# Hybrid S5 and gated-DeltaNet layer: 32x32 triangular blocks inverted on GpSimd, the decay matrix from a masked scan, and new operation durations in the model that places background work

## The chip, the cores and the metric

The kernel runs on one core of a Trainium2 chip. The metric is the device time of one execution in microseconds (us), as a median of several runs. The engines are TensorE (PE; its weight loads are listed apart as PEld), VectorE (DVE), ScalarE (ACT), GpSimd (POOL) and SyncE (SP), which issues most of the transfers between the chip's main memory (DRAM) and its on-chip memory.

## What is computed

The reference is one residual layer on x of 1024 rows by 2048 columns, in float32. Cut to what matters here:

```python
h = rmsnorm(x, ln_w)
proj = h @ w_in          # split: u_s, z_s (1024 each), q, k, v, z_d (1024 each), beta, a (8 each), gate_s, gate_d (2048 each)
# S5: 64 groups x 64 complex states, a linear recurrence along the rows, then GELU, GLU, SiLU gate
y_s = s5_mixer(u_s, z_s, ...) @ s5_w_up
# DeltaNet, 8 heads of 128: short convolution, SiLU, l2norm, then the chunked delta rule
decay = exp(where(causal, gc[:, None] - gc[None, :], -inf))      # gc = cumsum(g) in a chunk
a_mat = where(strict, beta[:, None] * (k @ k.T) * decay, 0)
sol = triangular_solve(I + a_mat, [v * beta, k * beta * exp(gc)])
y_d = ... @ dn_w_up
x = x + (sigmoid(gate_s) * y_s + sigmoid(gate_d) * y_d) @ w_out
out = rmsnorm(x, final_norm_w)
```

## The kernel before

**Passes and foreground.** The rows are worked in two passes of 512 (`NPASS`, `T`). In a pass the foreground is a stream of PE matmuls of 128x128 weights against 512 columns. Each weight chunk is split into a high and a low float32r part (`whi` by ACT, `wlo` by DVE, from `raw`, which SP loads), and the sum takes three matmuls per 128x128 block. `plan` lists the projection tiles in order: `ba`, then for each head the tiles k, q, v, z and two of gate_d with one S5 input tile `u` between, then the `zs` tiles, the DeltaNet up projection `ud`, the gate `gs`, the S5 GLU `glu`, the S5 up projection `us`, and the output projection. A tile of w_in takes 48 matmuls, one of `glu`, `ud` or `us` 24.

**Background and planner.** All else is written as Python generators in lanes (`lanes`): `epi`, `io`, `chain`, `prep`, `tab`, `s5`, `out`, `x`. After each three foreground matmuls `pump()` gives every lane one chance to emit its next step. `step()` decides with a clock that runs while the program is written: `Clock` and `Timed` charge each instruction a duration from `COST` and keep for each engine the modelled time, and for each piece of memory when it was last written and read. A step is emitted once the modelled PE clock has passed the time at which the step before has its result, and if DVE's clock isn't too far ahead of PE's. The result is a fixed order on each engine; the clock has no part in the run. Two rules matter below. `late(lane, h)` says that head h of `prep` or `chain` is overdue (by more than `LATE`, in heads, against `now`, the place in the plan); while one is, `step()` holds back `s5` and `tab` altogether:

```python
            elif lane in ("s5", "tab") and job[0] >= 0 and late_any():
                return
```

And `drain(lane)` emits all that a lane still holds, at once, in a row. It stands ahead of `ud` for `prep` and `chain`, and ahead of the first `glu` tile for `s5` (with the tables of `tab` interleaved), since `glu` multiplies the S5 result.

**S5** (`s5_gen`, `s5_table`). An S5 group t holds 4 pairs in 2 slots, 8 groups and 32 pairs in a pass. A slot has two pairs: PE makes the inputs of both in PSUM, then for each pair DVE rotates (two products, two sums), scans twice, rotates back (two products, two sums) and copies the carries; PE makes the slot's outputs and ACT copies them out of PSUM. In the first pass each pair also needs a table of cosines and sines (`s5_table`), made by DVE and ACT, and stored in `cs_d`. A group ends with GELU and a split into two parts, four stores to `yg_d`; after the eighth, `yg_load` loads all into the blocks `G0a` and `G0b`. The working tiles of S5 lie in `G0a` and `G0b` too.

**DeltaNet** (`d_views`, `gates_prep`, `d_prep`, `d_chain`). Four chunks of 128 rows are worked side by side. `gates_prep` makes the log decays `gt` for all heads. `d_prep(h)`, in lane `prep`, one head after another on shared tiles, makes the decay matrix E: GpSimd multiplies the high and low part of the log decays into a causal mask (`dhl`), PE sums with `after_r` (four matmuls of 256 columns), ACT takes the exponential. Then come the k by k and k by q products, `LU` (the strictly upper part of a_mat, transposed), and the inverse of the unit triangle: `LU` is stored to `lu_d`, 32 diagonal blocks of 16x16 are loaded one to a partition, GpSimd inverts them by 15 substitution steps of two operations each, the inverses and their transposes go out to `tu_d` and come back as `Tm` and `U`; PE then merges 16 to 32 (two steps of 16 and 32 matmuls of 32x32, with `off16` and `id32` between), 32 to 64 and 64 to 128. `d_chain(h)` runs the recurrence over the chunks.

In the profile nearly all instructions have the line of the helper in `Timed` that issues them (L135), so groups are told apart by their tiles: M holds DeltaNet's tiles, G0a and G0b those of S5, X and Y the foreground's inputs.

Of the kernel before, what the change touches and what calls it, by code (L numbers as in the profile page):

```python
# [36 lines left out]
P = 128  # L37
# [56 lines left out]
class Timed:  # L94
    def __init__(self, eng, key, clock):
        self.eng, self.key, self.clock = eng, key, clock

    def __getattr__(self, name):
# [4 lines left out]
        def g(*a, **k):  # L103
# [6 lines left out]
            if self.key == "PE":  # L110
                if name == "transpose":
                    c = 0.11
                elif k["rhs"].dtype == F32R:
                    c = n / 2400
                else:
                    rows = k["lhsT"].shape[0]
                    c = max(n / 600, 0.06) * (0.3 if o.shape[0] <= 32 else 0.5 if min(o.shape[0], rows) <= 64 else 1.0)
# [3 lines left out]
            else:  # L121
# [26 lines left out]
def kernel(  # L148
# [64 lines left out]
    def tt(o, a, b, op, eng=None):  # L213
        (eng or V).tensor_tensor(o, a, b, op=op)
# [24 lines left out]
    off16 = cpool.tile([P, 2, 16], F32, name="off16")  # L239
    id32 = cpool.tile([P, 32], F32, name="id32")  # L240
    G.memset(off16, 0.0)
    for b in range(4):
        s32 = slice(32 * b, 32 * b + 32)
        G.tensor_copy(id32[s32, :], ident[s32, s32])
        G.memset(off16[s32, 0, :], -1.0)
        G.affine_select(off16[s32, 0, :], off16[s32, 0, :], pattern=[[0, 16]], compare_op=ALU.is_ge,
                        fill=0.0, base=-16, channel_multiplier=1)
    after_r = cpool.tile([P, P], F32R, name="after_r")
    S.activation(after_r, after, AF.Copy)
# [27 lines left out]
    lu_d = [dram.tile([4, 129, P], F32, name=f"lu_d{i}") for i in range(2)]  # L277
    tu_d = [[dram.tile([4, 129, P], F32, name=f"tu_d{i}{j}") for j in range(2)] for i in range(2)]
# [718 lines left out]
    def d_views(mb):  # L997
# [19 lines left out]
    gth = cpool.tile([P, 8, 4], F32, name="gth")  # L1017
    gtl = cpool.tile([P, 8, 4], F32, name="gtl")
# [4 lines left out]
    def gates_prep(lg, ps_):  # L1023
# [50 lines left out]
    dhl = cpool.tile([P, 2, P], F32R, name="dhl")  # L1074
# [16 lines left out]
    def d_prep(h, ps_):  # L1091
# [6 lines left out]
        pD = bank(5)  # L1098
# [7 lines left out]
        S.activation(E.rearrange("p c n -> p (c n)"), pD, AF.Exp)  # L1106
# [39 lines left out]
        SP.dma_start(rows(lud), LU)  # L1146
        yield
        mif = mi.rearrange("p c n -> p (c n)")
        Ef = E.rearrange("p c n -> p (c n)")
        ba = mif[0:32, 0:256].rearrange("p (i m) -> p i m", i=16)  # L1150
        btm = mif[0:32, 256:512].rearrange("p (i m) -> p i m", i=16)
        bx = Ef[0:32, 0:256].rearrange("p (i m) -> p i m", i=16)
        bu = Ef[0:32, 256:512].rearrange("p (i m) -> p i m", i=16)
        SP.dma_start(ba, diag_blocks(lud))
        G.memset(mif[0:32, 256:512], 0.0)
        G.memset(mif[0:32, 256:512:17], 1.0)
# [10 lines left out]
        G.tensor_copy(bu, btm.rearrange("p i m -> p m i"))  # L1167
        yield
# [523 lines left out]
```

## Time and profile before

| | before |
|---|---|
| median of 3 runs | 2998.08 us (2997.61 to 3001.38) |
| the profiled execution | 3000.75 us |
| its span, first to last instruction | 2998.7 us |
| mean granted TensorE clock | 0.996 |
| DMA | 405.29 MB, 135 GB/s |
| busy: DVE, ACT, POOL | 1676.4, 1149.5, 460.2 us |

A busy share is that of the whole span. In a timeline a row gives the start, the length in us, the engine, the operation, the tile written and the tiles read, and in brackets how long the engine sat idle before it and for whom. In a table of groups stand the count, the busy time, the mean length in ns and the idle time ahead. In the first pass the last block of a head is worked on PE at 867 us, `ud` begins at 950 us and `glu` at 1216 us.

### The profile page before, as it was taken

The page shows a single profiled execution, that of the slowest core. Times are in us where ns is not written, and L with a number is a line of the kernel's source. Part 1 is how long each engine was busy: PE and PEld are TensorE (multiplying, and loading weights), DVE is VectorE, ACT ScalarE, POOL GpSimd, SP SyncE. Part 2 cuts the span into 40 slices and gives each one's busy share as a digit, 9 for nine tenths or more (in the row PEclk, how much of TensorE's full clock was granted, in tenths as well). Part 3 has the DMA queues.
Part 4 walks back from the last instruction along what each step waited for, and adds up shares of the span by engine and source line. Part 5 has one row for each costly group of instructions (what it writes and reads, how often), then busy time and mean ns, then how long its engine had stood idle before and what let it go on. Part 6 is the DMA issues. An engine that isn't in the chain of part 4 may idle for free.

```text
span 2998.7 us, 42470 instructions
## 1 busy us (share of the span) xinstructions
PE 2952.0 (98%) x15902; PEld 2372.9 (79%) x15902; DVE 1676.4 (56%) x3130; ACT 1149.5 (38%) x2483; POOL 460.2 (15%) x857
## 2 busy tenths in 40 slices
PE   8999999999999999999999999999999999999998
PEld 6877777777777888888878777777777788888887
DVE  5746777777767422553454676567556633226542
ACT  5434544554544222334333344333433322223331
POOL 4413222122200000000024221222122000000000
PEclk9999999999999999999999999999999999999999
DMA  6435445444545644446354444544444464445541
GB/s 166 125 79 145 115 131 135 112 123 122 135 136 161 195 119 119 145 137 239 120 162 133 116 116 117 137 120 115 123 127 122 137 198 123 118 125 155 195 149 57
DMA packets 618240, 405.29 MB, mean 135 GB/s; under 512 B 91257, under 2 KB 551218, under 8 KB 616114
## 3 DMA queue, kind: packets, MB, share of 16 engines
q1 hardware_dynamic: 615730, 394.19, 46.2%
q0 software_dynamic: 2304, 8.39, 0.8%
q8 instruction: 125, 2.05, 0.3%
q14 instruction: 81, 0.66, 0.1%
HBM read 335.79 MB, written 66.72 MB: 134 GB/s over the span
## 4 chain that ended last, share of the span: by engine, by line
PE 85%; DVE 6%; ACT 3%; POOL 2%; DMA 2%; issue 2%; SPq 1%; DVEq 0%; POOLq 0%; ACTq 0%
PE p L135 85%; DVE G0a L135 2%; DVE M L135 2%; POOL M L135 2%; DVE wlo L135 1%; ACT M L135 1%; DVE tmp L135 1%; SPq L135 1%; POOL smalls L135 1%; DMA M<-tu_d 0%; ACT tmp L135 0%; ACT whi L135 0%; ACT L135 0%; ACT G0b L135 0%; DMA raw<-in_w_in_dram 0%
## 5 line engine op out<-in xcount | busy, mean ns | idle before, releaser
L135 PE MATMUL p<-X,whi 128*128 128x512 f32 (+1 forms) x4432 | 1396.4, 397 | 1.5 <-DVE whi L135 0.8
L135 DVE TENSOR_TENSOR wlo<-raw,whi 128x512 fp32r<-128x512 f32 x920 | 633.2, 700 | 744.2 <-ACT whi L135 743.5
L135 PEld LDWEIGHTS p<-X,whi 128*128 128x128 f32 (+1 forms) x4432 | 802.0, 188 | 175.3 <-issue 17.9
L135 PE MATMUL p<-X,wlo 128*128 128x512 f32 (+1 forms) x2184 | 852.7, 390 | 0.3 <-DVE wlo L135 0.2
L135 ACT ACTIVATE whi<-raw 128x512 fp32r<-128x512 f32 x917 | 557.8, 625 | 519.0 <-PE p L135 487.2
L135 PE MATMUL p<-Y,whi 128*128 128x512 f32 (+1 forms) x1808 | 568.0, 396 | 0.9 <-ACT p L135 0.9
L135 PEld LDWEIGHTS p<-X,wlo 128*128 128x128 f32 x2184 | 410.9, 188 | 89.1 <-DVE wlo L135 0.9
L135 PEld LDWEIGHTS p<-Y,whi 128*128 128x128 f32 (+1 forms) x1808 | 330.7, 187 | 71.3 <-issue 3.9
L135 PE MATMUL p<-Y,wlo 128*128 128x512 f32 x896 | 349.7, 390 | 0.0
L135 POOL TENSOR_SCALAR smalls<-smalls 128x4 f32<-128x4 f32 (+1 forms) x58 | 18.2, 313 | 1584.8 <-DVE smalls L135 1116.3
L135 ACT ACTIVATE tmp<-p 128x512 f32<-128x512 f32 x160 | 95.5, 597 | 400.9 <-PE p L135 393.6
L135 POOL TENSOR_TENSOR M<-M 32x28 f32<-32x28 f32 (+8 forms) x492 | 196.7, 400 | 282.8 <-DMA M<-lu_d 200.1
L135 DVE TENSOR_TENSOR G0a<-G0a 128x256 f32<-128x256 f32 (+1 forms) x432 | 211.1, 525 | 7.2 <-ACT G0a L135 3.5
L135 PEld LDWEIGHTS p<-M 32*32 32x32 f32 (+2 forms) x3072 | 153.0, 123 | 72.6 <-ACT M L135 28.8
L135 PEld LDWEIGHTS p<-Y,wlo 128*128 128x128 f32 x896 | 168.1, 188 | 36.5 <-DVE wlo L135 0.4
L135 PE MATMUL p<-M 32*32 32x32 f32 (+3 forms) x3072 | 186.9, 215 | 6.9 <-DMA M<-tu_d 3.8
L135 ACT ACTIVATE M<-p 32x128 f32<-32x128 f32 (+3 forms) x337 | 98.9, 297 | 161.1 <-PE p L135 157.5
L135 DVE SCALAR_TENSOR_TENSOR tmp<-tmp,vec 128x512 f32<-128x512 f32 x144 | 112.0, 778 | 11.7 <-ACT tmp L135 8.3
L135 DVE TENSOR_TENSOR G0a<-p,G0a 128x512 f32<-128x512 f32 x128 | 82.0, 681 | 13.9 <-PE p L135 13.8
L135 DVE TENSOR_TENSOR_SCAN G0a<-rho,scar,G0a 128x256 f32<-128x256 f32 x128 | 89.3, 738 | 0.0
L135 PE MATMUL p<-whi,G0a 128*128 128x512 f32 x280 | 88.5, 391 | 0.0
L135 PE MATMUL p<-whi,X 128*128 128x512 f32 x256 | 82.2, 393 | 0.0
(209 smaller groups left out, 2640.7 us busy)
## 6 DMA issues: line engine op xcount, KB each, us to landing
raw<-in_w_in_dram SPq DMA_DIRECT2D x324, 512.0 KB, 4.0
raw<-in_w_out_dram SPq DMA_DIRECT2D x56, 512.0 KB, 4.0
raw<-in_dn_w_up_dram SPq DMA_DIRECT2D x32, 512.0 KB, 4.1
raw<-in_s_w_up_dram SPq DMA_DIRECT2D x32, 512.0 KB, 3.9
td_d<-tmp SPq DMA_DIRECT2D x32, 256.0 KB, 2.0
M<-tu_d SPq DMA_DIRECT2D x32, 256.0 KB, 3.2
cs_d<-G0a SPq DMA_DIRECT2D x32, 256.0 KB, 2.2
yg_d<-G0a SPq DMA_DIRECT2D x64, 128.0 KB, 2.4
```

The source lines that it names most:

```text
L135: return f(*a, **k)
```

## The change

Three things are changed.

1. **32x32 blocks on GpSimd.** `lu_d` now takes the four 32x32 diagonal blocks of each chunk (four small stores), and each block is loaded to 8 partitions, whole (`lb`, 1024 numbers a partition); the 32 columns of the unit matrix are dealt over the 8 partitions, 4 to each, from a stored copy `idg_d`. All 128 partitions work. 31 substitution steps of two GpSimd operations give the inverse, one store to `tu_d` and one load give `U`, and a DVE transposition by 32x32 blocks gives `Tm`. The merging of 16 to 32 on PE goes, with its two DVE products and eight ACT copies.
2. **Masked scan.** The log decays are stored once per pass in `g_d` as rows. `d_prep` loads a head's 512 to all partitions, four DVE scans of 128 columns (state + g, times a strict mask) make the sums, and ACT takes the exponential. The `dhl` products and the four matmuls go.
3. **Durations.** `COST` and `Timed` get other numbers.

```diff
                 elif k["rhs"].dtype == F32R:
-                    c = n / 2400
+                    c = n / 2400 + 0.0137
...
-_VG = {"V": (0.07, 1.04e-3), "G": (0.14, 2.1e-3), "S": (0.05, 0.9e-3)}
-_VF = {"V": (0.1, 0.6e-3), "G": (0.12, 1.1e-3), "S": (0.05, 0.9e-3)}
+_VG = {"V": (0.17, 1.04e-3), "G": (0.33, 1.95e-3), "S": (0.2, 0.82e-3)}
+_VF = {"V": (0.17, 0.6e-3), "G": (0.22, 1.3e-3), "S": (0.2, 0.82e-3)}
...
-        for j in range(2):
-            for i, gg in enumerate((gth, gtl)):
-                tt(dhl, gg[:, h, 2 * j:2 * j + 2].unsqueeze(2).broadcast_to([P, 2, P]),
-                   causal[:, None, :].broadcast_to([P, 2, P]), MUL, eng=G)
-                yield
-                PE.matmul(pD[:, j * 256:(j + 1) * 256], lhsT=after_r, rhs=dhl.rearrange("p c n -> p (c n)"),
-                          start=(i == 0), stop=(i == 1))
+        SP.dma_start(Ef, part(g_d, h * 512, (0, P), (1, 512)))
+        yield
+        for c in range(4):
+            V.tensor_tensor_scan(E[:, c, :], E[:, c, :], strict, 0.0, op0=ADD, op1=MUL)
...
-        for j in range(15):
-            n = 15 - j
-            a = ba[:, j, j + 1:16].unsqueeze(2).broadcast_to([32, n, j + 1])
-            b = btm[:, j:j + 1, 0:j + 1].broadcast_to([32, n, j + 1])
-            tt(bx[:, 0:n, 0:j + 1], a, b, MUL, eng=G)
-            tt(btm[:, j + 1:16, 0:j + 1], btm[:, j + 1:16, 0:j + 1], bx[:, 0:n, 0:j + 1], SUB, eng=G)
+        for j in range(31):
+            n = 31 - j
+            a = lb[:, j:j + 1, j + 1:32].broadcast_to([P, 4, n])
+            b = iu[:, :, j:j + 1].broadcast_to([P, 4, n])
+            tt(ix[:, :, 0:n], a, b, MUL, eng=G)
+            tt(iu[:, :, j + 1:32], iu[:, :, j + 1:32], ix[:, :, 0:n], SUB, eng=G)
...
-        SP.dma_start(diag_blocks(tud[0]), btm)
-        SP.dma_start(diag_blocks(tud[1]), bu)
+        SP.dma_start(part(tud, 0, (4128, 16), (512, 8), (P, 4), (1, 32)), iu)
...
-        SP.dma_start(Tm, rows(tud[0]))
-        SP.dma_start(U, rows(tud[1]))
+        SP.dma_start(U, rows(tud))
+        yield
+        V.transpose(Tm.rearrange("p c n -> p (c n)"), U.rearrange("p c n -> p (c n)"))
...
-                PE.matmul(pG[b, c * 32:(c + 1) * 32], lhsT=LU[b, c, b], rhs=Tm[b, c, b], start=True, stop=True)
...
-                PE.matmul(pU[b, c * 32:(c + 1) * 32], lhsT=g3[b, c, :], rhs=U[b, c, b], start=True, stop=True)
-                PE.matmul(pU[b, P + c * 32:P + (c + 1) * 32], lhsT=U[b, c, b], rhs=g3[b, c, :],
-                          start=True, stop=True)
```

The new durations move instructions. The first place is PE within one head of the first pass: p is a PSUM bank, M the block products of the triangle, X and whi or wlo the foreground. Before:

```order
L135 MATMUL p_677_5872<-M_64_533 32x32 x16
L135 MATMUL p_674_5858<-X_6_173,whi_5766 128x512 x2
L135 MATMUL p_674_5858<-X_6_173,wlo_5767 128x512
L135 MATMUL p_674_5858<-X_6_173,whi_5799 128x512 x2
L135 MATMUL p_674_5858<-X_6_173,wlo_5800 128x512
L135 MATMUL p_674_5858<-X_6_173,whi_5799 128x512 x2
L135 MATMUL p_674_5858<-X_6_173,wlo_5800 128x512
L135 MATMUL p_681_5909<-M_64_533 32x32 x32
```

And the same engine and step now:

```order
L142 MATMUL p_594_4902<-X_6_157,whi_4858 128x512 x2
L142 MATMUL p_594_4902<-X_6_157,wlo_4859 128x512
L142 MATMUL p_600_4935<-M_64_516 32x32 x8
L142 MATMUL p_594_4902<-X_6_157,whi_4858 128x512 x2
L142 MATMUL p_594_4902<-X_6_157,wlo_4859 128x512
L142 MATMUL p_594_4902<-X_6_157,whi_4858 128x512 x2
L142 MATMUL p_594_4902<-X_6_157,wlo_4859 128x512
L142 MATMUL p_601_4952<-M_64_516 32x32 x16
```

Before, the steps of 16 and 32 blocks merge 16 to 32, and a step of 8 follows. The step of 8 is now the first block step of a head; those of 16 and 32 ahead of it are gone. The second place is PE where `glu` begins in the first pass, behind the last `gs` tile. Before, with G0a read as the GLU's input:

```order
L135 MATMUL p_1294_10569<-X_7_174,whi_10570 128x512 x2
L135 MATMUL p_1294_10569<-X_7_174,wlo_10571 128x512
L135 MATMUL p_1306_10642<-G0a_9231,whi_10589 128x512 x2
L135 MATMUL p_1306_10642<-G0a_9231,wlo_10590 128x512
L135 MATMUL p_1306_10642<-G0a_9231,whi_10589 128x512 x2
```

The same place now (G0b alone, 128x256: inputs of an S5 slot; G0b with G0a, 128x256 and 64x256: its outputs):

```order
L142 MATMUL p_1255_10015<-X_7_158,wlo_10017 128x512
L142 MATMUL p_1267_10121<-G0b_2147 128x256
L142 MATMUL p_1268_10122<-G0b_2147 128x256
L142 MATMUL p_1267_10121<-G0b_2147 128x256
L142 MATMUL p_1268_10122<-G0b_2147 128x256
L142 MATMUL p_1269_10165<-G0b_2147,G0a_2146 128x256
L142 MATMUL p_1269_10165<-G0a_2146,G0b_2147 64x256 x4
L142 MATMUL p_1270_10180<-G0b_2147 128x256
L142 MATMUL p_1271_10181<-G0b_2147 128x256
L142 MATMUL p_1270_10180<-G0b_2147 128x256
L142 MATMUL p_1271_10181<-G0b_2147 128x256
L142 MATMUL p_1272_10228<-G0b_2147,G0a_2146 128x256
```

Two more slots of this kind follow before the first GLU matmul, `p_1282_10371<-G0a_10359,whi_10037`: the four slots of S5 groups 6 and 7 now stand here with no foreground between, where before they stood among the foreground ahead. The third place is DVE at that point now (rho and scar belong to the scans, fhi and flo to a table; wlo is the foreground's):

```order
L142 TENSOR_TENSOR G0a_2146<-p_1267_10121,G0a_2146 128x512 x2
L142 TENSOR_TENSOR G0a_2146<-G0a_2146 128x256 x2
L142 SCALAR_TENSOR_TENSOR G0a_2146<-rho,scar,G0a_2146 128x256 x2
L142 TENSOR_TENSOR G0a_2146<-G0a_2146 128x512 x2
L142 TENSOR_TENSOR G0a_2146<-G0a_2146 128x256 x2
L142 COPY G0a_2146<-scar 128x2
L142 COPY scar<-G0a_2146 128x2
L142 TENSOR_SCALAR G0a_2146<-G0a_2146,fhi 128x256
L142 TENSOR_SCALAR G0a_2146<-G0a_2146 128x256
L142 TENSOR_TENSOR G0a_2146<-G0a_2146 128x256
L142 SCALAR_TENSOR_TENSOR G0a_2146<-G0a_2146,flo 128x256
L142 TENSOR_TENSOR G0a_2146<-p_1268_10122,G0a_2146 128x512 x2
```

This is pair 24, the first half of a table, and the start of pair 25. In all, eight pairs and six tables of the first pass stand between the last `gs` matmul and the first of `glu`; before, none did.

More of the change, by code (lines that the diff above doesn't have):

```diff
@@ L113, in g @@
                 elif k["rhs"].dtype == F32R:
-                    c = n / 2400
-                else:
-                    rows = k["lhsT"].shape[0]
-                    c = max(n / 600, 0.06) * (0.3 if o.shape[0] <= 32 else 0.5 if min(o.shape[0], rows) <= 64 else 1.0)
+                    c = n / 2400 + 0.0137
+                    if self.apart:
+                        c += 0.09
+                        self.apart = False
+                else:
+                    part = min(o.shape[0], k["lhsT"].shape[0])
+                    c = 0.05 if part <= 32 else max(n / 960, 0.15) if part <= 64 else max(n / 600, 0.2)
+                    if part <= 64 and not self.apart:
+                        c += 0.1
+                    self.apart = True
                 lat = 0.1
@@ L238 @@
                     channel_multiplier=1)
[L239 to L249, printed above, removed]
+    afterk = cpool.tile([P, P], F32, name="afterk")
+    S.activation(afterk, after, AF.Copy)
+    strict = cpool.tile([P, P], F32, name="strict")
+    tt(strict, causal, ident, SUB, eng=G)
     halfpi = cpool.tile([P, 1], F32, name="halfpi")
@@ L275 @@
     cs_d = dram.tile([32, P, 512], F32, name="cs_d")
-    lu_d = [dram.tile([4, 129, P], F32, name=f"lu_d{i}") for i in range(2)]
-    tu_d = [[dram.tile([4, 129, P], F32, name=f"tu_d{i}{j}") for j in range(2)] for i in range(2)]
+    lu_d = [dram.tile([4, 4, 1024], F32, name=f"lu_d{i}") for i in range(2)]
+    tu_d = [dram.tile([4, 129, P], F32, name=f"tu_d{i}") for i in range(2)]
+    idg_d = dram.tile([1, 32, 32], F32, name="idg_d")
+    g_d = dram.tile([1, 32, P], F32, name="g_d")
     nq_d = [dram.tile([1, P, 16], F32, name=f"nq_d{i}") for i in range(2)]
@@ L1062, in gates_prep @@
         gf = gt.rearrange("p h t -> p (h t)")
-        S.activation(gth.bitcast(F32R), gt, AF.Copy)
-        tt(gtl, gt, gth, SUB, eng=G)
         p3 = bank(5)
-        for i, m in enumerate((causal, after_r.bitcast(F32), ones)):
+        PE.transpose(p3[0:32, 96:96 + P], gf, ident)
+        for i, m in enumerate((causal, afterk, ones)):
             PE.matmul(p3[:, i * 32:(i + 1) * 32], lhsT=m, rhs=gf, start=True, stop=True)
+        grow = mif[0:32, 256:256 + P]
+        S.activation(grow, p3[0:32, 96:96 + P], AF.Copy)
+        SP.dma_start(g_d[0], grow)
         exf = ex.rearrange("p a n -> p (a n)")
@@ L1072, in gates_prep @@
         yield -1
-    dhl = cpool.tile([P, 2, P], F32R, name="dhl")
     nk = [small(f"nk{i}", 4) for i in range(2)]
@@ L1145, in d_prep @@
         yield
-        SP.dma_start(rows(lud), LU)
+        for b in range(4):
+            SP.dma_start(part(lud, b * 1024, (32, 32), (4096, 4), (1, 32)),
+                         LU[32 * b:32 * b + 32, :, 32 * b:32 * b + 32])
         yield
[L1148 to L1156, printed above, removed]
-        yield
-        for j in range(15):
-            n = 15 - j
-            a = ba[:, j, j + 1:16].unsqueeze(2).broadcast_to([32, n, j + 1])
-            b = btm[:, j:j + 1, 0:j + 1].broadcast_to([32, n, j + 1])
-            tt(bx[:, 0:n, 0:j + 1], a, b, MUL, eng=G)
-            tt(btm[:, j + 1:16, 0:j + 1], btm[:, j + 1:16, 0:j + 1], bx[:, 0:n, 0:j + 1], SUB, eng=G)
+        lb = dw["Emi"].rearrange("p (j t) -> p j t", j=32)
+        Uf = U.rearrange("p c n -> p (c n)")
+        iu, ix = (Uf[:, i * P:(i + 1) * P].rearrange("p (m t) -> p m t", m=4) for i in range(2))
+        SP.dma_start(dw["Emi"], part(lud, 0, (1024, 16), (0, 8), (1, 1024)))
+        SP.dma_start(Uf[:, 0:P], part(idg_d, 0, (0, 16), (P, 8), (1, P)))
+        yield
+        for j in range(31):
[4 more added lines that the diff above has]
+            tt(iu[:, :, j + 1:32], iu[:, :, j + 1:32], ix[:, :, 0:n], SUB, eng=G)
             if j % 3 == 2:
                 yield
-        G.tensor_copy(bu, btm.rearrange("p i m -> p m i"))
-        yield
-        SP.dma_start(diag_blocks(tud[0]), btm)
-        SP.dma_start(diag_blocks(tud[1]), bu)
+        SP.dma_start(part(tud, 0, (4128, 16), (512, 8), (P, 4), (1, 32)), iu)
         stored = clock.last
@@ L1323, in zero_tu @@
     def zero_tu():
-        for a in tu_d:
-            for b in a:
-                SP.dma_start(rows(b), ztile.rearrange("p (c n) -> p c n", c=4))
+        for b in tu_d:
+            SP.dma_start(rows(b), ztile.rearrange("p (c n) -> p c n", c=4))
+        SP.dma_start(idg_d[0], ident[0:32, 0:32])
     def out_gen(yr, oss, r0):
```

37 lines of the change are left out of this document (9 added, 28 removed).

## The prediction

> **What bounds the kernel now.** I read the page first: how long, which engine, and the chain that ended last.
>
> ```profile
> span 2998.7 us, 42470 instructions
> PE 2952.0 (98%) x15902; PEld 2372.9 (79%) x15902; DVE 1676.4 (56%) x3130; ACT 1149.5 (38%) x2483; POOL 460.2 (15%) x857
> PE 85%; DVE 6%; ACT 3%; POOL 2%; DMA 2%; issue 2%; SPq 1%; DVEq 0%; POOLq 0%; ACTq 0%
> ```
>
> TensorE (PE) is busy for 98% of the span and carries 85% of the chain. Whatever the other engines do is free as long as PE never waits for it. So two things have to be priced: PE instructions that go or come, and PE waits that go or come. The second view is the busy time by stretches, for PE's pace where it has the projections alone; the other row is for later.
>
> ```profile
> 290.80:294.10 3.30, 3.30 (x10) 2.82 (x11) 3.27 (x7) 1.41 (x5) 0.00 (x0) 0.50 0.06 10
> 1050.00:1125.00 75.00, 75.00 (x333) 62.10 (x332) 18.69 (x28) 20.31 (x35) 0.00 (x0) 1.00 0.44 121
> ```
>
> 333 matmuls of 512 columns in 75.00 us are 0.225 us each. That is my ruler: where background work stands between two projection matmuls, it costs PE the distance of their starts less 0.225 us. The third view is PE's timeline in one head of the delta rule and one S5 slot.
>
> ```profile
> 560.33 0.39 PE L135 MATMUL p<-X,wlo 128*128 128x512 f32 x1
> ...
> 560.68 0.63 PE L135 MATMUL p<-X,whi 128*128 128x512 f32 x2
> ...
> 612.86 0.39 PE L135 MATMUL p<-X,wlo 128*128 128x512 f32 x1
> ...
> 614.62 0.73 PE L135 MATMUL p<-X,whi 128*128 128x512 f32 x2
> ...
> 619.78 0.39 PE L135 MATMUL p<-X,wlo 128*128 128x512 f32 x1
> ...
> 621.16 0.73 PE L135 MATMUL p<-X,whi 128*128 128x512 f32 x2
> ...
> 624.47 0.39 PE L135 MATMUL p<-X,wlo 128*128 128x512 f32 x1
> 624.79 0.89 PE L135 MATMUL p<-M 32*32 32x32 f32 x32
> 625.61 0.73 PE L135 MATMUL p<-X,whi 128*128 128x512 f32 x2
> ...
> 627.56 0.39 PE L135 MATMUL p<-X,wlo 128*128 128x512 f32 x1
> 627.87 1.91 PE L135 MATMUL p<-M 32*32 32x32 f32 x64
> 629.71 0.73 PE L135 MATMUL p<-X,whi 128*128 128x512 f32 x2
> ```
>
> Between the first two rows stands one decay matmul (it reads dhl); between the next two an S5 slot's output matmuls; between 619.78 and 621.16 an S5 slot's input matmuls. The rows of 32 and 64 records are the two 32x32 steps that the change removes; a float32 matmul leaves two records.
>
> **What PE loses.** The 32x32 steps cost 625.61 - 624.47 - 0.225 = 0.92 and 629.71 - 627.56 - 0.225 = 1.93 us, and the projection pair behind each takes 0.73 instead of 0.63, 0.10 more. Per head that is 3.05 us, for 16 heads (8 in each of two passes) 48.8 us. The decay matmuls cost 560.68 - 560.33 - 0.225 = 0.125 us each.
>
> ```profile
> L135 PE MATMUL p<-dhl,after_r 128*128 128x256 f32 x64 | 20.6, 322 | 1.6 <-POOL dhl L135 1.6
> ```
>
> There are 64: 8.0 us. Together PE sheds 56.8 us; one transposition per pass comes back, under 1 us.
>
> **What lies beside PE.** The four masked scans and the 32x32 transposition give VectorE (DVE) some 2 us per head and the two products with off16 and id32 go; ScalarE (ACT) loses eight small copies. DVE is busy for only 56% of the span, beside PE's stream, so I take nothing; without that cover, if each head waited for DVE, it were 16 x 2 = 32 us. SP issues nine transfers per head instead of six; at 0.6 us an issue (the yg_d rows below) that is 1.8 us per head, with weight loads queued behind, and its store of the inverse waits for GpSimd. Three weight buffers feed 24 matmuls each, 16 us of PE, so this is hidden too.
>
> **GpSimd's chain** grows from 30 dependent operations to 62.
>
> ```profile
> 600.92 14.21 POOL L135 TENSOR_TENSOR M<-M 32x15 f32<-32x15 f32 x30 [17.89 <-DMA M<-lu_d]
> ```
>
> ```profile
> M<-tu_d SPq DMA_DIRECT2D x32, 256.0 KB, 3.2
> ```
>
> At 14.21 / 30 = 0.47 us each, 62 take 29.4 us. Ahead of them the last load must land, behind them a store, the load of the inverse (3.2 us) and the transposition come: with 2.4 us for each of the other transfers (the yg_d row below) and 0.7 for a 512-wide operation, 38.1 us. In the changed order 179 to 220 projection matmuls stand between the issue of that last load and PE's first block step: 40.3 to 49.5 us, and the background work between comes on top, by the rows above some 4 us. So PE need not wait: cost 0, with the second rival as the other end.
>
> **What the new durations move** is the main term. The planner lets no S5 step start while a head's preparation is late. With 62 costlier GpSimd steps modelled, the preparation lane needs nearly a whole head, is late most of the time, and the S5 lane of the first pass starves: its fifth pair of 32 stands behind projection matmul 2585 (before: 1111), and pairs 24 to 31 still stand undone when the GLU projection must begin. There the code drains the lane. The eight pairs, six tables and the GELUs of groups 5 to 7 come in one row, and PE's next projection reads their result. Nothing covers that. Before, the last group was stored 950 matmuls ahead of this point. The view by tile of the S5 tiles, for an S5 stretch with little else on DVE, gives minimum / median / maximum ns:
>
> ```profile
> L135 DVE TENSOR_TENSOR G0a<-G0a x15: 416/421/692, 906.4 to 943.7; 128x256 f32<-128x256 f32 x10, 128x512 f32<-128x512 f32 x5
> ...
> L135 DVE TENSOR_TENSOR_SCAN G0a<-rho,scar,G0a x6: 725/734/746, 904.5 to 944.7; 128x256 f32<-128x256 f32 x6
> L135 DVE TENSOR_SCALAR G0a<-G0a x4: 293/294/294, 909.5 to 928.7; 128x256 f32<-128x256 f32 x4
> L135 DVE TENSOR_TENSOR G0a<-p,G0a x4: 681/685/691, 911.3 to 942.2; 128x512 f32<-128x512 f32 x4
> L135 ACT ACTIVATE G0a<-G0a x4: 401/516/632, 911.6 to 932.0; 128x256 f32<-128x256 f32 x2, 128x512 f32<-128x512 f32 x1, 128x512 fp32r<-128x512 f32 x1
> L135 DVE SCALAR_TENSOR_TENSOR G0a<-G0b x4: 416/417/421, 915.6 to 928.9; 128x256 f32<-128x256 f32 x4
> L135 SPq DMA_DIRECT2D yg_d<-G0a x4: 576/600/616, 933.4 to 935.3; - x4
> L135 DVE COPY G0a<-scar x2: 159/160/162, 908.8 to 919.7; 128x2 f32<-128x2 f32 x2
> ...
> L135 DVE SCALAR_TENSOR_TENSOR G0a<-G0a,flo x2: 485/485/485, 910.3 to 921.8; 128x256 f32<-128x256 f32 x2
> L135 ACT ACTIVATE G0b<-G0a x2: 417/418/418, 911.3 to 922.3; 128x256 f32<-128x256 f32 x2
> L135 ACT ACTIVATE G0b<-G0a,halfpi x2: 510/511/512, 912.1 to 923.0; 128x256 f32<-128x256 f32 x2
> ...
> L135 DVE SCALAR_TENSOR_TENSOR G0a<-G0a,G0b x2: 684/685/686, 929.2 to 931.3; 128x512 f32<-128x512 f32 x2
> ```
>
> A pair is two products from PSUM (0.69), four 256-wide sums (0.42), two scans (0.73), two 512-wide products (0.69) and two copies (0.16): 6.2 us on DVE. A table is 1.5 us on DVE, 0.42 + 0.40 + 0.51 = 1.3 us on ACT, then 1.1 us on DVE. A GELU with its split is three ACT (0.63) and three DVE operations (0.69): 4.0 us. The input matmuls of a slot are 1.38 - 0.225 = 1.15 us, its outputs 1.76 - 0.225 = 1.54. The copy out of PSUM and the transfers:
>
> ```profile
> 926.02 0.38 ACT L135 ACTIVATE G0b<-p 128x256 f32<-128x256 f32 x1 [2.46 <-PE p L135]
> ```
>
> ```profile
> yg_d<-G0a SPq DMA_DIRECT2D x64, 128.0 KB, 2.4
> G0a<-yg_d POOLq DMA_DIRECT2D x10, 512.0 KB, 8.4
> G0b<-yg_d POOLq DMA_DIRECT2D x6, 512.0 KB, 12.6
> ```
>
> ```profile
> 1001.64 2.94 POOL L135 DMA_DIRECT2D G0a<-yg_d  x5 [135.89 <-DMA tmp<-td_d]
> ```
>
> The chain in which PE stands still: the last gate's tanh 0.6, group 5's GELU 4.0, four stores (3 x 0.6 + 2.4 = 4.2, since the next pair overwrites their source): 8.8. A slot with two tables: 2 x 6.2 + 1.5 + 1.1, then the next table's first half 1.5, its ACT part 1.3 ahead of the copy 0.4, and the next inputs 1.15: 19.4. Group 6: 19.4 + 18.3 (no inputs behind it) + 4.0 + 4.2 = 45.9. Group 7: 19.4, its last slot without tables 12.4 + 0.8 + 0.4, then 4.0 + 4.2: 41.2. Eight loads at 0.59 us an issue: the last is issued at 4.1 and lands 12.6 later, 16.7, plus three matmuls, less the 24 x 0.225 = 5.4 us that the first tile takes anyway: 12.0. Sum 107.9 us. For handoffs I add 2. A hole also slows what follows: behind PE's wait of 2.5 us at 288 the row of 290.80 above shows a granted clock of 0.50 and 10 matmuls in 3.30 us, where the ruler gives 14.7. The 4.2 us of PE work inside the chain would double: 4 more. I take 114 us, bounds 95 (operations overlapping better) and 135.
>
> The Trainium skill, in "TensorE: Matmul & The Clock Gate", section "What's actually happening", says that the array's clock falls to half after about 3.4 us idle and rises again after about 3.4 us of work; this trace agrees on the half, after a hole of only 2.5 us. By that rule alone every PE step in the drain is at half rate, which is what I added; without it the sum is 4 us lower.
>
> The four slots' matmuls leave the stream for that chain: 4 x (1.15 + 1.54) = 10.8 us less there. PE's other idle time is 2998.7 - 2952.0 = 46.7 us, part of it the start; truer durations should place steps a little later than their inputs: -10, from -25 to +15.
>
> **Sum.** -56.8 - 10.8 + 1 + 114 - 10 = +37 us. The profiled execution took 3000.75 us, so 3038; it lies 2.7 above the median of 2998.08, which makes 3035 beside that median.
>
> **Rivals.** *The drain runs at DVE's pace.* If the pairs and tables overlap all that ACT, PE and SP do, the stall is 8 x 6.2 + 6 x 2.6 + 12.0 = 77 us, and if the other waits fall by 25 the sum is -56.8 - 10.8 + 1 + 77 - 25 = -15: 2983, faster. It decides from a stall under some 77 us, with my -10. For it: DVE's work is 65 of the 108. Against: one A and B buffer, and the GELU uses them too, so groups cannot overlap. Chance 0.07.
>
> *GpSimd's chain is late.* Contention shows in the trace: a DVE operation beside a long GpSimd memset.
>
> ```profile
> 13.47 0.75 DVE L135 TENSOR_SCALAR M<-M,smalls 128x1024 f32<-128x1024 f32 x1
> 26.17 3.97 DVE L135 TENSOR_SCALAR M<-M,smalls 128x1024 f32<-128x1024 f32 x1 [0.44 <-POOL smalls L135]
> ```
>
> ```profile
> 26.09 3.50 POOL L135 MEMSET G0a<- 128x4096 f32 x1
> ```
>
> The same shape takes 3.97 instead of 0.75 us. If the new 128-partition steps lose as well and take 0.70 us, chain and transfers need 62 x 0.70 + 8.7 = 52.1 us where the order leaves some 195 x 0.225 + 4 = 47.9: 4.2 us x 16 heads = 67 us of new PE waits, 3102. It decides from 0.58 us a step, where the shortest head's 44.3 us are used up. Against: the 30 steps of the row ran beside DVE too. Chance 0.13. The Trainium skill, in "GPSIMD Engine Reference", section "Key points", says that GpSimd shares its SBUF interfaces with VectorE and contends with instructions in a two-port mode or with two SBUF inputs; the rows above agree for the first kind.
>
> The forecast has the other 0.80, with its own range 3012 to 3062.
>
> **How the numbers follow.** The range of 3010 to 3080 leaves out the first rival and most of the second. A measurement here tells 0.2% (6 us) from no change. Faster by more: the first rival's 0.07 less a little, 0.05. Within: 0.04, where a short drain just pays. Slower: 0.91.
>
> **What would show it.** Right: one PE hole of 95 to 135 us (in pieces, with the S5 matmuls between) about 1216 us in, where `glu` began before, DVE busy in it and the granted clock at 0.50; S5 tiles nearly absent from DVE in the first heads; in the second pass every head shorter by some 3.5 us. Wrong: no such hole, or PE waits for tu_d in every head, or GpSimd steps over 0.58 us.

## The result, and the profile after

The changed kernel takes 3031.11 us as a median of 4 runs (3029.5 to 3032.55), the kernel before 2999.02 beside it (4 runs, 2997.61 to 3001.38). The ratio is 1.0106, with a 95% interval of 1.0089 to 1.0124: it is slower by 1.1%, and lies 4 us under the forecast. The profiled execution took 3032.55 us, 31.8 more than that of before.

The page of the changed kernel first, with the rows that stood at the head of the prediction:

```profile
span 3030.1 us, 39679 instructions
...
PE 2899.7 (96%) x14304; PEld 2336.3 (77%) x14304; DVE 1712.5 (57%) x3178; ACT 1120.8 (37%) x2357; POOL 633.6 (21%) x1243
...
PE 85%; DVE 3%; POOL 1%; ACT 1%; DMA 1%; issue 0%; SPq 0%; DVEq 0%; POOLq 0%; ACTq 0%
```

PE is busy for 52.3 us less, and the kernel is still longer: PE now stands idle for 3030.1 - 2899.7 = 130.4 us, before for 46.7. Nearly all of the new idle time is in one place. PE's timeline there, from the last `gs` matmuls to the first GLU tile:

```profile
1180.62 0.40 PE L142 MATMUL p<-X,wlo 128*128 128x512 f32 x1
1180.94 1.13 PE L142 MATMUL p<-G0b 64*128 64x256 f32 x8
1192.45 1.19 PE L142 MATMUL p<-G0b,G0a 128*128 128x256 f32 x2 [10.37 <-issue]
...
1204.97 1.97 PE L142 MATMUL p<-G0a,G0b 128*64 128x256 f32 x6 [7.15 <-DVE G0a L142]
1208.31 2.08 PE L142 MATMUL p<-G0b 64*128 64x256 f32 x8 [1.37 <-ACT G0b L142]
...
1227.66 2.08 PE L142 MATMUL p<-G0b 64*128 64x256 f32 x8 [1.37 <-ACT G0b L142]
...
1254.08 2.08 PE L142 MATMUL p<-G0b 64*128 64x256 f32 x8 [1.36 <-ACT G0b L142]
...
1283.74 1.22 PE L142 MATMUL p<-G0a,whi 128*128 128x512 f32 x2 [14.24 <-DMA G0a<-yg_d]
...
1293.98 0.39 PE L142 MATMUL p<-G0b,wlo 128*128 128x512 f32 x1
```

For 1283.74 - 1180.62 - 0.225 = 102.9 us no projection matmul starts. The rows between, 16 in full, are S5's: four slots, each with its inputs (64x256) and outputs (128x256). Behind the hole the 24 matmuls of the first GLU tile take 10.24 us from the first start to the last where the ruler gives 23 x 0.225 = 5.2, since the transfers of their input land one by one and the first six matmuls still run at half rate: 5.1 more, 108.0 in all. The busy times in the hole, in the stretch of `ud` that was the ruler before, and in the first GLU tile (the columns are the stretch, PE, PEld, DVE, ACT and POOL busy, the granted clock, DMA share and GB/s):

```profile
1181.50:1284.00 102.50, 24.16 (x71) 10.14 (x68) 67.42 (x150) 21.25 (x39) 4.36 (x8) 0.52 0.20 62
1050.00:1125.00 75.00, 75.00 (x343) 59.96 (x342) 47.89 (x99) 36.74 (x59) 0.00 (x0) 1.00 0.50 145
1284.00:1293.00 9.00, 7.49 (x21) 4.01 (x21) 0.42 (x1) 0.00 (x0) 0.18 (x1) 0.81 0.99 360
```

DVE works for 67 of the 102 us, ACT for 21, PE at a granted clock of 0.52. In the `ud` stretch DVE is busy for 47.89 us where it had 18.69: 33.1 us of it are S5 work of the starved lane that came late, where before there was none. From 300 to 500 us, in the first heads, S5's tiles take 5 us of DVE instead of 72.

The chain on GpSimd, SP's issues around it and PE's first block step, in the third head:

```profile
348.46 0.55 SPq L142 DMA_DIRECT2D M<-lu_d  x1
...
353.03 33.46 POOL L142 TENSOR_TENSOR M<-M 128x124 f32<-128x124 f32 x62 [6.04 <-DMA M<-idg_d]
...
386.51 0.56 SPq L142 DMA_DIRECT2D tu_d<-M  x1
...
389.41 0.37 SPq L142 DMA_DIRECT2D M<-tu_d  x1
...
394.83 0.70 DVE L142 STREAM_TRANSPOSE M<-M 128x512 f32<-128x512 f32 x1
...
396.80 0.39 PE L142 MATMUL p<-X,wlo 128*128 128x512 f32 x1
397.12 0.59 PE L142 MATMUL p<-M 32*32 32x32 f32 x16
397.64 0.73 PE L142 MATMUL p<-X,whi 128*128 128x512 f32 x2
```

PE finds the inverse ready 1.6 us ahead and does not wait: 397.64 - 396.80 - 0.225 = 0.62 us for the step. The 62 operations took 33.46 us, 0.54 each.

Two waits are new that no part of the prediction had; the first comes with the durations, since the kernel before with the new durations alone has it too (11.2 us). S5's setup is drained in a row ahead of the first `u` tile, and weight parts queue behind it on DVE; and DVE waits for GpSimd's power of 96 columns in the second pass (`ex`, from the gates), with weight parts behind that wait:

```profile
230.07 14.59 DVE L142 TENSOR_TENSOR Y<-Y 128x1024 f32<-128x1024 f32 x12
244.57 2.49 DVE L142 TENSOR_TENSOR wlo<-raw,whi 128x512 fp32r<-128x512 f32 x4
245.32 0.79 PE L142 MATMUL p<-X,wlo 128*128 128x512 f32 x1 [10.76 <-DVE wlo L142]
...
1648.22 16.03 POOL L142 TENSOR_TENSOR ex<-e,ex 128x96 f32<-128x96 f32 x1 [1.60 <-DVE ex L142]
1664.28 0.69 DVE L142 TENSOR_TENSOR M<-p,ex 128x512 f32<-128x512 f32 x1 [9.07 <-POOL ex L142]
1666.38 0.80 PE L142 MATMUL p<-Y,wlo 128*128 128x512 f32 x1 [2.83 <-DVE wlo L142]
```

### The profile page after: what moved, and what is told of

It is laid out like the page before. It is cut to its first block, busy times and chain, and to the rows that moved or that the text cites. A ratio compares the mean times of both kernels' runs of the same rounds, so it can differ in the third digit from the quotient of the medians.

```text
span 3030.1 us, 39679 instructions
## 1 busy us (share of the span) xinstructions
PE 2899.7 (96%) x14304; PEld 2336.3 (77%) x14304; DVE 1712.5 (57%) x3178; ACT 1120.8 (37%) x2357; POOL 633.6 (21%) x1243
## 4 chain that ended last, share of the span: by engine, by line
PE 85%; DVE 3%; POOL 1%; ACT 1%; DMA 1%; issue 0%; SPq 0%; DVEq 0%; POOLq 0%; ACTq 0%
PE p L142 85%; DVE G0a L142 2%; POOL M L142 1%; POOL ex L142 1%; DVE M L142 0%; DMA G0b<-yg_d 0%; DMA yg_d<-G0a 0%; ACT G0a L142 0%; DMA raw<-in_w_in_dram 0%; ACT L142 0%; DVE wlo L142 0%; ACT G0b L142 0%; SPq L142 0%; ACT M L142 0%; POOL smalls L142 0%
## 5 line engine op out<-in xcount | busy, mean ns | idle before, releaser
L142 DVE TENSOR_TENSOR wlo<-raw,whi 128x512 fp32r<-128x512 f32 x920 | 640.9, 708 | 631.7 <-ACT whi L142 630.6
L142 POOL TENSOR_TENSOR M<-M 128x32 f32<-128x32 f32 (+30 forms) x1004 | 445.9, 444 | 175.9 <-DMA M<-idg_d 97.1
L142 PEld LDWEIGHTS p<-M 32*32 32x32 f32 (+2 forms) x1536 | 111.9, 139 | 48.0 <-issue 16.6
L142 PE MATMUL p<-M 32*32 32x32 f32 (+3 forms) x1536 | 137.8, 237 | 2.0 <-ACT M L142 1.4
L142 ACT ACTIVATE M<-p 32x128 f32<-32x128 f32 (+3 forms) x195 | 55.7, 290 | 121.7 <-PE p L142 113.7
L142 POOL TENSOR_TENSOR M<-M,causal 128x512 f32<-128x512 f32 x16 | 21.2, 1326 | 372.6 <-ACT M L142 349.4
```

Of the source, the lines that this page charges most:

```text
L142: return f(*a, **k)
```

## The experiments

The theory: the loss is the S5 backlog that the planner builds up (new durations and its rule for late heads) and drains at the GLU. The rivals: GpSimd's longer chain costs, by contention or by being late; or the durations cost by themselves. The kernel before was run beside each group, 2999.1 to 3000.3 us; the ratios are to it, with 95% intervals.

### The rule that holds S5 back taken out (e1_no_gate)

```diff
-            elif lane in ("s5", "tab") and job[0] >= 0 and late_any():
-                return
```

> The changed kernel without the planner's rule that holds back the S5 lane while a preparation is late; blocks, scan and durations stay. In its order the last S5 group of the first pass is stored 310 projection matmuls ahead of the first GLU matmul (changed kernel: three groups at the GLU itself), 70 us. Theory A (the loss is the drained S5 backlog): the hole of 103 us and the 4 us behind it go, four slots' matmuls return to the stream, +10.8: 3031 - 107 + 11 = 2935, from 2920 to 2950, faster than before. Rival B (the rule protected the heads; S5 beside a longer preparation makes PE wait for tu_d or LU): 1 to 4 us of new waits in each of 8 heads, 2943 to 2967, and rows of PE waiting for DVE or GpSimd behind M. Rival C (the backlog was not what cost): 3020 or more.

Measured: 2941.68 us, ratio 0.981 (0.9796 to 0.9825). From the page and the list of PE's waits:

```profile
PE 2889.8 (98%) x14304; PEld 2338.6 (79%) x14304; DVE 1701.4 (58%) x3178; ACT 1124.1 (38%) x2361; POOL 644.7 (22%) x1243
...
PE p L142 <- DVE M L142: 20.8, 8, 5.2
PE p L142 <- DVE wlo L142: 13.8, 3, 10.7
```

Two lines less are worth 89 us. Idle time falls from 130.4 to 2943.6 - 2889.8 = 53.8 us, with blocks, scan and durations as they were. Theory A holds; the time is 7 us above its middle. Of the waits for M some 11 us are at the ends of the first heads' recurrences, which come at their deadlines (6 us in the changed kernel). That is the kind of wait that rival B had, and at most these few us are left for it.

### Old durations, with and without the rule (e2_old_durations, e6_old_no_gate)

The changed kernel with the durations of before:

```diff
-                    c = n / 2400 + 0.0137
+                    c = n / 2400
...
-_VG = {"V": (0.17, 1.04e-3), "G": (0.33, 1.95e-3), "S": (0.2, 0.82e-3)}
+_VG = {"V": (0.07, 1.04e-3), "G": (0.14, 2.1e-3), "S": (0.05, 0.9e-3)}
...
```

> The changed kernel's blocks and scan, with the durations of the kernel before. Its last S5 group of the first pass is stored 590 projection matmuls ahead of the GLU: no drain. Theory A (shed on PE 57 us by the prediction, about 66 with the stalls at the removed steps; nothing else of the two edits costs): 2999 - 57 to 66 = 2933 to 2942. Rival B (old durations take the 62 GpSimd steps for shorter than they are, so block steps are placed too early and PE waits for the inverse): the model charges a step 0.14 + 0.0021 x 62 + 0.16 = 0.43 us on average where the profile has 0.44, so no more than 1 us per head, 16 us: up to 2958. Rival C (the new chain costs by contention on GpSimd and VectorE): steps over 0.58 us, 2990 or more.

> Blocks and scan with the durations of before, and without the rule that holds back the S5 lane: the partner of the run with new durations and no rule (2941.7). Theory A (the rule plays no part here; the old durations place the block steps too early, and PE waits some 3 us in each of 16 heads at the first 32x32 step and behind it): 2990 to 3010, first block step at a median above 2 us instead of 0.61. Rival B (part of the 60 us between the two runs so far is the rule, which also held back S5 in the run with old durations): below 2980.

Measured: 3001.37 us with the rule (ten executions, from 2990.5 to 3011.2; ratio 1.0004, 0.9992 to 1.0016), 3012.56 without (1.0043, 1.003 to 1.0056). There is no drain in either, and yet nothing is gained. The first run has rival C's time without its sign (its slowest chain takes 0.54 us a step from start to start, not over 0.58); theory A and rival B as priced are over 40 us too low. The second is 3 us above the range of its theory A. The head of the run with the rule whose row answers to the one shown above:

```profile
317.10 0.55 SPq L136 DMA_DIRECT2D M<-lu_d  x1
...
321.80 33.48 POOL L136 TENSOR_TENSOR M<-M 128x124 f32<-128x124 f32 x62 [3.95 <-DMA M<-idg_d]
...
355.31 0.57 SPq L136 DMA_DIRECT2D tu_d<-M  x1
357.51 0.37 SPq L136 DMA_DIRECT2D M<-tu_d  x1
...
360.31 0.71 DVE L136 STREAM_TRANSPOSE M<-M 128x512 f32<-128x512 f32 x1 [7.13 <-DMA M<-tu_d]
...
361.08 0.87 PE L136 MATMUL p<-M 32*32 32x32 f32 x16 [4.62 <-DVE M L136]
```

Here the chain runs without slack: SP's store waits for the last operation, and from the load's issue to PE's step it takes 361.08 - 317.10 = 44.0 us. PE waits 4.62 us, and then runs at half rate (a granted clock of 0.55 over the next 5 us). The first block step costs 2.5 us at the median, instead of 0.61, in the 14 heads where it stands alone between two projection matmuls. My bound of 1 us per head came from the mean busy time of an operation, 0.44 us; from start to start it is 33.48 / 62 = 0.54, which makes 62 x 0.10 = 6 us per head. So rival B holds in kind, several times dearer than I had it; the partner without the rule, with a median of 2.4 us at that step, says that the rule has no part in it. From its page (span 3007.9 us):

```profile
PE 2928.6 (97%) x14304; PEld 2355.5 (78%) x14304; DVE 1705.5 (57%) x3178; ACT 1113.7 (37%) x2357; POOL 625.9 (21%) x1243
```

Beside the run with new durations and no rule, PE's idle time is 3007.9 - 2928.6 = 79.3 us instead of 53.8, and its busy time, for the same 14304 matmuls, 2928.6 instead of 2889.8: waits and slower running make up the 64 us between the two.

### One duration, and the durations alone (e3_short_gpsimd, e4_new_durations)

```diff
-_VG = {"V": (0.17, 1.04e-3), "G": (0.33, 1.95e-3), "S": (0.2, 0.82e-3)}
+_VG = {"V": (0.17, 1.04e-3), "G": (0.17, 1.95e-3), "S": (0.2, 0.82e-3)}
```

> The changed kernel with one number changed: the fixed part of a GpSimd tensor_tensor 0.17 instead of 0.33 us, which with the 0.16 of latency makes 0.45 us for the mean step (the profile has 0.44). The S5 lane catches up; its last group is stored 20 to 41 projection matmuls ahead of the GLU, 5 to 9 us. Theory A (the one duration starves the lane): the hole shrinks to what the loads of the GLU's input need beyond that, 16.7 - 7 = about 10 us with a few us of half clock: 2935 + 12 = 2947, from 2935 to 2965. Rival B (it is the other durations or the length of the chain as such): hole over 50 us, 2985 or more.

Measured: 2973.5 us (four executions, from 2969.5 to 2985.9; 0.9928, 0.9905 to 0.9951), above theory A's range. The hole is gone as it said (some 8 us are left, at the transfers of the GLU's input and in its first tile), but the block steps wait again, as in the runs before. From PE's waits:

```profile
PE p L142 <- DVE M L142: 29.3, 12, 5.2
```

So the one number 0.33 both starves S5 and gives the block steps their slack. The kernel before with the new durations alone:

> The kernel before with the new durations alone: 16x16 blocks, decay matmuls and all PE work as before. Its last S5 group of the first pass is stored 356 projection matmuls ahead of the GLU: no drain, so the durations alone do not starve the lane. Theory A (durations only move waits): the prediction gave -10, from -25 to +15, for them: 2989, from 2974 to 3014. Rival B (the new durations cost by themselves, by placing steps late and draining prep ahead of the up projection): over 3014.

Measured: 2983.93 us (0.9949, 0.9934 to 0.9964), -15.5 us beside 2999.41: within theory A. From its page:

```profile
PE 2938.4 (99%) x15902; PEld 2372.6 (80%) x15902; DVE 1674.4 (56%) x3130; ACT 1148.7 (39%) x2483; POOL 466.8 (16%) x857
```

Most of the gain is in PE's busy time: 2952.0 - 2938.4 = 13.6 us less for the same 15902 matmuls. Durations, structure and rule together (an empty field was not run alone):

| | rule | no rule |
|---|---|---|
| old structure, old durations | 2999.4 | |
| old structure, new durations | 2983.9 | |
| new structure, old durations | 3001.4 | 3012.6 |
| new structure, new durations | 3031.1 | 2941.7 |

Of these the new structure gains only with the new durations and without the rule, and the new durations cost only with the new structure and the rule.

### Half the backlog (e9_later_rule)

```diff
-LATE = (1.0, 1.4)
+LATE = (1.4, 1.8)
```

> The changed kernel with the rule that holds S5 back loosened: a preparation counts as late from 1.4 heads behind instead of 1.0, a recurrence from 1.8 instead of 1.4. In its order half as much is drained at the first GLU matmul: the GELU of group 6 and all of group 7 (4 pairs, 2 tables; 68 DVE operations instead of 147). Theory A (the hole is the backlog's chain, with the prediction's pieces): tail of group 6 8.8, group 7 41.2, first tile's loads 12.0, handoffs and half clock 3: hole and what stands behind it 62 to 65 us where the changed kernel has 107; two slots' matmuls are out of the stream instead of four; beside the run without the rule (2941.7) 2941.7 + 63 - 5 = 2999, from 2988 to 3008. Rival B (what costs is any stop of the stream, loads and half clock, whatever the backlog): hole of 90 us or more, 3020 or more. Rival C (the hole falls more than in proportion): below 2980.

Measured: 2985.46 us (0.9954, 0.9941 to 0.9968), 2.5 under the range of theory A. The hole in its timeline:

```profile
1180.69 0.40 PE L142 MATMUL p<-X,wlo 128*128 128x512 f32 x1
1181.02 1.14 PE L142 MATMUL p<-G0b 64*128 64x256 f32 x8
...
1208.32 2.08 PE L142 MATMUL p<-G0b 64*128 64x256 f32 x8 [1.36 <-ACT G0b L142]
...
1238.11 1.22 PE L142 MATMUL p<-G0a,whi 128*128 128x512 f32 x2 [14.37 <-DMA G0a<-yg_d]
```

It is 1238.11 - 1180.69 - 0.225 = 57.2 us, 45.7 less than in the changed kernel. The group that is no longer drained was priced at 45.9. The hole is the backlog's chain, piece by piece; rivals B and C fall. The whole time is 14 lower than I made it; 7 of that are waits for M at the ends of recurrences (13.8 us in its list of PE's waits, 20.8 in the run without the rule).

### The scan alone (e5_scan_only)

The kernel before with new durations and the masked scan (the diff is the second hunk of the change).

> The kernel before with the new durations (run with those alone: 2983.9) and the masked scan, but the 16x16 blocks and the merge of 16 to 32 on PE. Theory A (the decay matmuls cost PE 64 x 0.125 = 8 us, and one of them waited 1.9 us for dhl): 2984 - 8 to 11 = 2973 to 2976. Rival B (the scans on VectorE and the transfers on SP delay the weight parts): PE waits for wlo or M grow by as much, 2980 to 2988. What is left to the run with both edits and no rule for the S5 lane (2941.7) is then the share of the 32x32 blocks: about 33 by theory A, where 48.8 us of PE work go.

Measured: 2991.22 us (nine executions, from 2985.5 to 2998.1; 0.9975, 0.9966 to 0.9985), 7 above the run without the scan, outside both ranges. The 64 decay matmuls are gone, and other waits came: 2.82 us at 1597 for wlo behind the power (the new wait shown for the changed kernel at 1666), 3.8 us for the recurrence's state, 2.0 for S5's G0b. The scan alone does not pay here; which of its shifts costs how much was not taken apart.

### Mending the other waits (e7, e8, e10, e11)

The run without the rule still had its 10.7 us wait at 234. The first attempt (e7) let the setup run further ahead and waited for the gates' last step; the second (e8) had 0.27 for GpSimd's fixed part as well.

```diff
-SETUP = 2.0
+SETUP = 4.0
...
         gts(negc, ex[:, 0, :], -1.0, 0.0, MUL, ADD)
-        yield -1
+        yield
```

> The changed kernel without the rule for the S5 lane, with the S5 setup allowed to run 4 us of DVE ahead instead of 2 (so it is done before the first u tile drains it) and with the gates' last step waited for (the power of 16 us on GpSimd that VectorE waited for). Theory: the wait of 10.7 us at 234, its half clock of about 3 us, and about 3 us at 1578 go: 2942 - 14 to 17 = 2925 to 2928, from 2918 to 2932. Rival (the setup's VectorE work moves to earlier places where PE waits for the weight parts as well): 2935 to 2945.

> As the run with setup and gates mended, and the fixed part of a GpSimd tensor_tensor 0.27 instead of 0.33 us: 62 x 0.06 = 3.7 us less planned for each head's chain, and with it an earlier recurrence. Theory A (the 0.33 is more than the chain needs; PE waits of 11 us at the ends of the first heads' recurrence shrink, block steps still find their inverse): 2915 to 2928. Rival B (the slack of the block steps, some 3.5 us between the load of the inverse and PE by the rows, is what keeps PE from waiting; 3.7 us less eats it): a wait of 0.5 to 2 us in each head at the first 32x32 step, 2930 to 2955.

Measured: 3051.0 us (1.0173, 1.016 to 1.0187) and 2987.69 us (0.9962, 0.9949 to 0.9975): misses, of over 100 and of over 30 us above even the ranges of their rivals. PE's timeline of e7 at the end of a head's `k` tile, and the stretch's busy times:

```profile
445.80 0.40 PE L142 MATMUL p<-X,wlo 128*128 128x512 f32 x1
448.45 0.59 PE L142 MATMUL p<-M 32*32 32x32 f32 x16 [2.25 <-DVE smalls L142]
...
453.80 1.22 PE L142 MATMUL p<-state,M 128*128 128x128 f32 x4
...
475.40 1.12 PE L142 MATMUL p<-ident,M 128*128 128x128 f32 x4 [3.48 <-DVE M L142]
476.17 1.20 PE L142 MATMUL p<-X,whi 128*128 128x512 f32 x2
```

```profile
445.80:475.60 29.80, 16.96 (x107) 12.55 (x106) 6.30 (x18) 6.92 (x24) 1.42 (x3) 0.59 0.10 29
```

For 30 us PE has no projection matmul: the inverse's merging and the whole recurrence of head 2 stand in a row, because the code drains `prep` and `chain` of head h - 2 at that tile. Five heads of the first pass go this way in e7, and in e8 six recurrences in part, each with an end like the one at 475.40. It is the same mechanism as at the GLU, in another lane: the first heads start later, the lanes need nearly all the time that they are given, and a delay is never made up, only drained at each deadline. GpSimd's first two chains start at 151 and 292 us, in the run without the rule at 131 and 262. In e7 the setup may run 4 us of DVE ahead and the preparation only 3, so the setup goes first; but the wait for the gates' step holds up the first preparation too, and no run separates the two. Both turned round (preparation and recurrence 8, setup 3; the gates' step waited for in the second pass only):

```diff
...
-    slack = {"epi": 99.0, "io": 99.0, "chain": 4.0, "prep": 3.0, "s5": 1.0, "tab": 1.0, "out": 3.0, "x": 3.0}
+    slack = {"epi": 99.0, "io": 99.0, "chain": 8.0, "prep": 8.0, "s5": 1.0, "tab": 1.0, "out": 3.0, "x": 3.0}
...
```

> The changed kernel without the rule for S5; S5's setup may run VectorE 3 us ahead, the preparation and the recurrence 8 us (so they rank ahead of the setup; in the run with 4 for the setup and 3 for the preparation, the setup held the heads up, and five heads were drained at their deadlines). The gates' last step is waited for in the second pass. In the order no head and no part of the setup's long row is drained. Theory: the 11 us wait at 234 with its half clock, the 11 us at the ends of the first heads' recurrence, and 3 us at 1578 go: 2941.7 - 15 to 27 = 2915 to 2927. Rival (VectorE further ahead for the heads means weight parts queued behind them: waits for wlo and whi in each head): 2935 to 2960.

> The changed kernel without the rule for S5, the fixed part of a GpSimd tensor_tensor 0.29 instead of 0.33 us, the gates' last step waited for in the second pass; limits of the lanes as in the changed kernel. In the order no head is drained; half of the setup's long row still is. Theory: the waits at the ends of the first heads' recurrence (11 us) and 3 us at 1578 go, the wait at 234 is halved; block steps stand 62 x 0.04 = 2.5 us earlier, within their slack of some 3.5 us: 2920 to 2932. Rival (the block steps have less slack in some heads: 1 to 2 us a head): 2935 to 2955.

Measured: 2928.49 us (0.9762, 0.9749 to 0.9776) and, with the lanes' limits as they were and 0.29 for GpSimd, 2932.72 us (0.978, 0.9766 to 0.9793), each about 1 us above its range. The first is the fastest version, 2.4% under the kernel before. Its page:

```profile
span 2927.7 us, 39618 instructions
...
PE 2886.5 (99%) x14304; PEld 2335.1 (80%) x14304; DVE 1703.7 (58%) x3178; ACT 1129.3 (39%) x2363; POOL 664.9 (23%) x1243
```

### The control to the fastest run (e12_control)

The kernel before with the same durations, limits and rule-free planner, so that only blocks and scan are left between the two.

> The control to the fastest run (2928.5): the kernel before, with 16x16 blocks, the merge on PE and the decay matmuls, but with the new durations, no rule for S5, the same limits of the lanes and the gates' last step waited for in the second pass. Only the two structural edits are left between the two. Theory A (the prediction's shed, 48.8 us of 32x32 steps and 8.0 of decay matmuls, less what placement gives back): 2928.5 + 57 = 2985, from 2970 to 2990, so that the planner's own repairs bring the old structure nothing over the 2984 that it had with new durations, or up to 14 (its wait of 11 us at 238 and the half clock behind). Rival B (much of the gain of the fastest run is the planner's, and the structure is worth half of the shed): 2945 to 2965.

Measured: 2974.5 us (0.9915, 0.9902 to 0.9929). Its page:

```profile
span 2971.9 us, 42502 instructions
...
PE 2939.0 (99%) x15902; PEld 2373.5 (80%) x15902; DVE 1682.4 (57%) x3130; ACT 1154.0 (39%) x2487; POOL 457.7 (15%) x857
```

In the fastest run PE is busy for 2939.0 - 2886.5 = 52.5 us less, and the span is 2971.9 - 2927.7 = 44.2 shorter: 8 us come back as idle time. Theory A's range holds. Of the 71.8 us from the kernel before (3000.28 beside this run, 2999.37 beside the fastest, so read to 1 us) to 2928.49, 46.0 are the structure's under a planner that places it well, and 25.8 the planner's.

## Why the prediction held, point by point

- **The drain** (114 us, 95 to 135). 108.0 measured, with what stands behind it. By PE's input steps the pieces are 27.4, 19.4, 26.4 and 29.7 us, then 5.1 behind; forecast were 8.8 + 19.4 = 28.2, 26.5, 19.4 and 33.8. The two in the middle come in the other order, since the inputs of group 7 go ahead of group 6's GELU. The transfers of the GLU's input cost 4.1 us from the first load's issue (1279.63) to PE's start and 5.1 behind, 9.2 (forecast 12.0); the last GELU with its stores took 9.7 (forecast 8.2), with a load of an ACT table, 1.28 us, that no term had. The pieces made 107.9 before the 6 us for handoffs and half clock. That 108.0 meets this is in part luck: the half clock does show (2.08 us for a slot's inputs in the hole, 1.13 ahead of it), and other pieces were shorter by as much. That the hole is the backlog is shown by two runs: without the rule the hole is gone, with half the backlog it is 45.7 us shorter.
- **The clock in the hole.** 0.52 granted. The Trainium skill, "TensorE: Matmul & The Clock Gate", section "What's actually happening", puts the change to half at about 3.4 us idle; the row agrees on the half. The waits of 10.4 and 14.2 us in the hole are longer than that, but behind the wait of 2.83 us at 1666 the granted clock was 0.50 as well (from 1666.4 to 1668.4), so here a shorter wait was enough.
- **Shed and other waits** (-56.8 + 1 - 10 = -65.8). 31.8 - 108.0 + 10.8, the slots that left the stream, gives -65.4. That the sum is right is luck: it holds two errors that offset. The setup's drained row and the power's wait, 10.76 + 2.83 = 13.6 us of PE waits, were in no term. And PE's busy time outside the hole fell by 2952.0 - 10.8 - (2899.7 - 24.2 - 3.6) = 69.3 us (24.2 lie in the hole, some 3.6 in the extra time of the first GLU tile) instead of 55.8; it fits that the durations alone take 13.6 us off PE's busy time. The other idle time fell as forecast: 130.4 less 78.3 in the hole, 1.5 in the first GLU tile and 13.6 leaves 37.0, before it was 46.7.
- **The shed by itself** (56.8). Its rows were right (the control still has 0.92 and 1.93 us per head); between control and fastest run 46.0 arrive, and of the missing 11 some 8 are idle time of PE; what caused it was not taken apart. The heads of the second pass were to be 3.5 us shorter; by the spacing of the stores to `zd_d` they are 91.8 us apart instead of 100.1, partly since S5's groups come later there too (in 200 us from shortly behind the first of these stores, 32 us of DVE instead of 52). With the old durations they are 100.1 again, in the control 98.2, in the fastest run 93.3.
- **The durations** ("truer durations should place steps a little later": -10, from -25 to +15). On the old structure -15.5. But this term was taken as independent of the structure, and there the step failed: with the old durations the new structure gains nothing (3001.4). Without the rule, and so without the backlog, the durations are worth 71 us to it (3012.6 against 2941.7).
- **GpSimd's chain** (38.1 us; cost 0; decides at 0.58 us a step). Cost 0 was right for this order, on a thinner margin than stated: without slack it takes 44.0 us. The working took the step of the old chain, 0.47, where the new one has up to 0.58 (below). Nor did waits begin at the deciding point in every order: in the run without the rule one head's chain took 37.15 us, 0.60 a step, and its first block step still cost 0.61 us. The second rival's mechanism is real; the order had room for it, and in e2 it had not.
- **The first rival**, a drain at DVE's pace, would have made 77 us: DVE was busy for 67 of the hole's 102.5 us and waited for the rest.

## What to carry to other kernels

A static order made from a model of durations has cliffs where a lane is nearly full: there a longer entry makes the lane late, a rule for late work starves another, and the bill comes as one drain at a deadline. Look for the drains in the order first, and price what stands in their row; then compare a structural edit under an order made for it, and give the old structure the same planner. Price a dependent chain by its time from start to start under the load that it will have, not by the mean busy time.

## What the runs showed of the hardware

GpSimd's chain is slower where DVE is busier. In the changed kernel the same 62 operations take, in a head of the second pass and in one of the first beside S5:

```profile
2132.03 29.07 POOL L142 TENSOR_TENSOR M<-M 128x124 f32<-128x124 f32 x62 [11.20 <-DMA M<-idg_d]
...
519.25 35.75 POOL L142 TENSOR_TENSOR M<-M 128x124 f32<-128x124 f32 x62 [4.57 <-DMA M<-idg_d]
```

```profile
2132.00:2161.00 29.00, 29.00 (x135) 22.96 (x134) 14.36 (x23) 8.51 (x15) 24.19 (x62) 1.00 0.52 142
519.30:555.00 35.70, 35.70 (x160) 29.54 (x159) 29.69 (x47) 17.37 (x33) 30.93 (x63) 1.00 0.41 110
```

With DVE busy for 50% of the time it is 0.47 us from start to start, with 83% it is 0.58. Over the 16 chains of this run the two go together (correlation 0.75), but not one for one: with the old durations one chain took 33.73 us, 0.54 a step, beside a DVE busy for 96%. The Trainium skill, "GPSIMD Engine Reference", section "Key points", says that GpSimd contends with DVE instructions that have two SBUF inputs; the rows agree in direction, and no run here separates such instructions from others. A power on GpSimd takes 16.03 us for 96 columns, so one `ex` holds up whoever reads it first.
